# VectorE and ScalarE in the written order in two stages of a two-block transformer on one core

## The chip, the cores and the metric

The kernel runs on one core of a Trainium2 chip. The metric is the device time of one execution in microseconds (us): the median of repeated runs, lower is better.

## What is computed

A chain of eight sub-layers on 256 tokens of width 1024 in f32: sparse attention, an MLP, forgetting attention, an MLP, a short convolution, an expert layer, differential attention and a second expert layer (`peer`, called twice). The change lies in the two expert layers. Each has 16,384 experts, addressed by two halves of 128 keys; a token takes 16 experts for each of 8 heads:

```python
def chunk(xc):
    q = (xc @ w_q).reshape(PEER_CHUNK, PEER_HEADS, 2, PEER_HALF)
    s = jnp.einsum('thpd,pnd->thpn', q, sub_keys)
    sv, si = lax.top_k(s, PEER_TOPK)
    cand_s = (sv[:, :, 0, :, None] + sv[:, :, 1, None, :]).reshape(...)
    cand_i = (si[:, :, 0, :, None] * PEER_KEYS + si[:, :, 1, None, :]).reshape(...)
    top_s, pos = lax.top_k(cand_s, PEER_TOPK)
    idx = jnp.take_along_axis(cand_i, pos, axis=-1)
    g = jax.nn.softmax(top_s, axis=-1)
    act = jax.nn.gelu(jnp.einsum('td,thkd->thk', xc, u[idx]), approximate=False)
    return jnp.einsum('thk,thkd->td', g * act, v[idx])
```

## The kernel before, in words

**Weights.** The weights of all stages stream through one queue of chunks of 128x1024 f32 (512 KB). SP's queue loads each into a `raw` buffer (three, and a fourth where the stage has room). `Weights.prep` (L296-319) splits a chunk into two parts: ScalarE casts the high part `whi` (L316), VectorE subtracts it from `raw` for the low part `wlo` (L317). `next` prepares up to three chunks ahead of the one in use. TensorE's `prod` multiplies a chunk in 24 matmuls: eight k-blocks of `whi` with the high and the low part of the activations (L527, L528: 16), then eight of `wlo` with the high part (L530). So a chunk needs the ScalarE cast first, and the VectorE difference only after 16 matmuls.

**The expert layer.** `begin` normalizes the input and makes the first four products early, while the normalization's factors are still computed; their results are corrected by `right` (L1399, L1419, tile `bo`). `peer_route` then multiplies 16 query chunks (`raw<-w_pq`, 256 tokens wide), and behind each of them two chunks of the experts' first matrix (`raw<-u`, `u_chunk`, 224 tokens wide; the last 32 tokens go by gathers of rows). 128 such chunks are needed; `u_chunk` applies the GELU to the result on ScalarE (L1810; once gates are there also L1817 with a product on VectorE, L1818). The query result is copied (L1760), its scores follow on TensorE one product later (`score`, L1750), and for every second query, that is for a head, ScalarE copies the scores to `sc` (L1753). Behind the third query, ScalarE adds the residual (L1279).

**The selection** is a generator in the background: each `project` lets it go on by one step, behind its product. A head takes six steps: `best` (L1654 to L1658: maximum, index, replacement, maximum, index on VectorE) for each of two token halves and two key halves, and per token half a step that forms candidate sums (L1671, L1672) and picks the best of them. Behind the eight heads comes `choose` for each token half in 14 steps: the softmax (L1685 to L1709, Exp on ScalarE), and the picked indices by comparison, product and sum on tiles of 128x1024 (L1718, L1721, L1722), four times; then three transposes on TensorE (L1730) and copies. `u_chunk` is called until the generator is done.

**Behind it** come the gates (L1919 to L1953) for the first 224 tokens, beside the remaining first-matrix chunks, and a side generator `gathered` (L1864 to L1916) that gathers rows for the last 32 tokens on POOL's queue and sums them on VectorE (L1893, L1907; these keep their own order by `keep_in_program_order`).

**The value stage.** For each of 128 chunks of the second matrix (`raw<-v`, `SA<-v`), `split` casts the row of gated activations into a high part (ScalarE L1973) and a low part (VectorE L1974), one row ahead, and TensorE multiplies it with the chunk in 8 matmuls of 448 columns and 8 of 224 (L2017) into eight banks.

**What sets the order.** The kernel is written as one stream of instructions. A scheduler orders each engine's share of it by its own estimates of durations and dependencies; the stream's order binds it only through data and buffers, and where the kernel pins instructions. Each engine runs its queue in the order that results. `manual_schedule(engines=...)` is a region of that scheduler: within it, each engine of the set issues its instructions in the order written. Other engines (TensorE, POOL, SP), the order across engines, and the place of the region's instructions among those of the same engine from outside, stay the scheduler's.

Of the kernel before, what the change touches and what calls it, by code (L numbers as in the profile page):

```python
# [32 lines left out]
LAMBDA_INIT = 0.8 - 0.6 * math.exp(-0.3)  # L33
NEG = -1e30
PER_Q = 2

GATHER = (32, 32)

# [316 lines left out]
class Kernel:  # L355
# [1281 lines left out]
    def peer_route(self, l, x, n_in, it, jt, g1, g2, pool, u_chunk, picked):  # L1637
# [22 lines left out]
        def tops():  # L1660
            for h in range(8):
                sc = scs.pop(h)
                for t in range(NT):
                    for p in range(2):
                        best(sv[t][:, 2 * h + p], si[t][:, 2 * h + p], sc[:, t, p])
                        yield


                    v0, v1 = sv[t][:, 2 * h], sv[t][:, 2 * h + 1]
                    cand = pw.tile([128, 136], F32, name="cand", bufs=2)  # L1670
                    nc.vector.tensor_scalar(cand[:, 0:16], v1, v0[:, 0:1], None, op0=ALU.add)  # L1671
                    nc.vector.tensor_add(cand[:, 16:].rearrange("p (r c) -> p r c", c=8),  # L1672
                                         v0[:, 1:16, None].to_broadcast([128, 15, 8]),
                                         v1[:, None, 0:8].to_broadcast([128, 15, 8]))
                    best(tss[t][:, h], poss[t][:, h], cand)
                    yield
            for t in reversed(range(NT)):
                yield from choose(t)
# [76 lines left out]
        for hp in range(16):  # L1755
# [5 lines left out]
            self.at(1, score, hp, q)  # L1761
            for _ in range(PER_Q):
                u_chunk()
            if hp == 1:
                self.background(tops(), 6 / (2 + 2 * PER_Q))

    def peer(self, l, inp):
# [4 lines left out]
        x, n_in = inp  # L1772
# [3 lines left out]
        with ExitStack() as es:  # L1776
            self.phase(g=4, f=4)
            with ExitStack() as s1:
# [4 lines left out]
                it = p0.tile([128, ND, 2], F16, name="it")  # L1783
                jt = p0.tile([128, ND, 2], F16, name="jt")
                g1 = p0.tile([128, ND, 2], F16, name="g1")
                g2 = p0.tile([128, ND], F32, name="g2")
# [17 lines left out]
                def u_chunk():  # L1804
                    j = done[0]
                    z = self.project(x, 0, ND)
                    tg = gated[0]
                    s = SA[:, j] if j < J3 else SB[:, j - J3]
                    if tg < ND:
                        nc.scalar.activation(s[:, tg:], z[:, tg:ND], AF.Gelu)  # L1810
                    if tg:
                        if tg < ND:
                            y = pact.tile([128, ND], F32, name="act", bufs=2)
                        else:

                            y = (it, jt)[j % 2].rearrange("p t a -> p (t a)").bitcast(F32)
                        nc.scalar.activation(y[:, :tg], z[:, :tg], AF.Gelu)  # L1817
                        nc.vector.tensor_mul(s[:, :tg], y[:, :tg], s[:, :tg])  # L1818
                    done[0] += 1

                with ExitStack() as s2:
                    self.lnp = self.wk = self.pool("pel", 1, stack=s2)
                    self.begin(inp)
                    self.w.widen(s2, count=60)
                    pr = self.pool("per", 1, stack=s2)
                    self.iota = self.const(pr, "iota")
                    nc.vector.tensor_copy(iof, self.iota)
                    self.peer_route(l, x, n_in, it, jt, g1, g2, pr, u_chunk, picked)
                    while self.bg is not None:
                        u_chunk()  # L1830
                        if self.bg_done:
                            self.bg = None
                    self.flush_tails()
                    assert self.w.used >= self.w.limit
                p3 = self.pool("pe3", 1, stack=s1)
                SB = p3.tile([128, NJ - J3, ND], F32, name="SB")
# [132 lines left out]
                def split(j):  # L1969

                    s = SA[:, j] if j < J3 else SB[:, j - J3]
                    c = pw.tile([128, 2, ND], F32R, name="c", bufs=3)
                    nc.scalar.copy(c[:, 0], s)  # L1973
                    nc.vector.tensor_sub(c[:, 1], s, c[:, 0])  # L1974
                    return c.rearrange("p a t -> p (a t)")


                cs = [split(0)]
                while done[0] < NJ:
                    u_chunk()  # L1980
# [3 lines left out]
                def added(m):  # L1984
                    add(m, ((out[m][:, 0:ND], 0), (out[m][:, ND:2 * ND], 0), (out[m][:, 2 * ND:2 * ND + G], ND)))
# [10 lines left out]
                for j0 in range(NJ - last + 1):  # L1996
                    if j0 == NJ - 8:
                        self.side_end()

                        inp = (self.xtile("xa"), 2) if l == 0 else None  # L2000
                        add = self.norm_tiles(1 + 2 * l, inp)
                    else:
                        self.tick()
                    if j0 == 24:
                        self.w.lengthen(self.wk, 2, NJ - j0)
                    js = range(j0, j0 + 1 if j0 < NJ - last else NJ)
                    ws = []
                    for j in js:
                        if j < NJ - 1:
                            cs.append(split(j + 1))  # L2010
                        ws.append(self.w.next())

                    def piece(i, part, m, start, stop):
                        o = out[m]
                        wm = ws[i][part][:, m * 128:m * 128 + 128]
                        n = 2 * ND - part * ND
                        nc.tensor.matmul(o[:, :n], wm, cs[i][:, :n], start=start, stop=stop, skip_group_check=True)  # L2017

                    if len(js) == 1:
                        for part in range(2):  # L2020
                            for m in range(KT):
                                piece(0, part, m, j0 == 0 and part == 0, False)
                        cs.pop(0)
                    else:
                        for m in range(KT):
                            for i in range(last):
                                for part in range(2):
                                    piece(i, part, m, False, i == last - 1 and part == 1)
                            if m > 0:
                                self.step()  # L2030
                                added(m - 1)
# [8 lines left out]
    def build(self):  # L2040
        nc, a = self.nc, self.a

        def w(name):
            return [a[name][j] for j in range(a[name].shape[0])]
# [4 lines left out]
        def wu(l):  # L2049
            q, u = w(f"w_pq{l}"), w(f"u{l}")  # L2050
            return [c for i in range(16) for c in [q[i]] + u[i * PER_Q:(i + 1) * PER_Q]] + u[16 * PER_Q:]

# [59 lines left out]
```

## Time and profile before

| | us |
|---|---|
| median of 3 runs (lowest, highest) | 2671.16 (2669.37, 2672.81) |
| the profiled execution | 2667.2 |
| its span in the trace | 2665.4 |
| TensorE busy in the span | 2550.9 |
| VectorE busy | 2061.5 |
| ScalarE busy | 1491.8 |
| routing of the first expert layer (first products to the last step of the choice) | about 855 to 1082 |
| routing of the second | about 1845 to 2070 |
| value stages begin at | about 1318 and 2305 |

The span is the time from the first to the last instruction in the trace. A busy TensorE (PE) includes matmuls at the lower clock. In the rows below, PEld is TensorE's weight load, DVE is VectorE, ACT is ScalarE, POOL is GpSimd and SP is SyncE; `wlo<-raw,whi` reads "tile wlo computed from raw and whi", L317 is a line of the kernel, x4 is a count of instructions, and a bracket at the end of a row gives the idle time of the engine ahead of it and what ended that.

### The profile page before, as it was taken

Reading aid. Unit: us, or ns where it says so; the run is one execution under the profiler, and the core shown is the slowest. Engines: PE = TensorE matmul, PEld = TensorE weight load, DVE = VectorE, ACT = ScalarE, POOL = GpSimd, SP = SyncE. Lnnn points to the kernel's source line nnn. Section 1 sums busy time; section 2 is a strip of 40 time slices with the busy share of each in tenths; the row PEclk is TensorE's granted clock in tenths of the full one; section 3 lists DMA queues with packets and bytes.
Section 4 is the critical chain, followed back from the end, with each engine's and each line's share of the span. In section 5 each row is a group of like instructions: output and inputs, shape, how many; then the busy total and the mean of one; then the engine's idle time right before and its main releaser. Section 6 shows DMA issues by size and latency. Waiting matters only on the chain. (4 is left out here: it accounts for less than half of the span.)

```text
span 2665.4 us, 50896 instructions
## 1 busy us (share of the span) xinstructions
PE 2550.9 (96%) x19696; PEld 2413.5 (91%) x19696; DVE 2061.5 (77%) x4181; ACT 1491.8 (56%) x3008; POOL 220.1 (8%) x150
## 2 busy tenths in 40 slices
PE   8999999989999998999899999999988999999997
PEld 7689998889999898899899998888988999889997
DVE  7678776588778886699878876768886699777786
ACT  5556455455455444588545554666444688545554
POOL 0000000000000000000023330000000000122320
PEclk9999999999999998999999999999998999999999
DMA  5148775378874454566688885332544666688882
GB/s 174 48 137 272 271 252 182 97 238 286 283 264 142 150 183 136 181 201 197 198 299 302 305 291 166 126 105 96 174 151 144 205 200 195 217 294 307 295 292 91
DMA packets 151955, 542.82 MB, mean 204 GB/s; under 512 B 17360, under 2 KB 20368, under 8 KB 151712
## 3 DMA queue, kind: packets, MB, share of 16 engines
q1 hardware_dynamic: 132600, 472.04, 53.8%
q0 software_dynamic: 18816, 67.25, 7.2%
q8 instruction: 154, 2.52, 0.4%
q14 instruction: 89, 0.73, 0.1%
q10 hardware_dynamic: 296, 0.28, 0.0%
HBM read 538.39 MB, written 1.11 MB: 202 GB/s over the span
## 5 line engine op out<-in xcount | busy, mean ns | idle before, releaser
L316 ACT CAST whi<-raw 128x1024 fp32r<-128x1024 f32 x715 | 749.0, 1048 | 761.3 <-PE g L528 321.3
L317 DVE TENSOR_TENSOR wlo<-raw,whi 128x1024 fp32r<-128x1024 f32 x715 | 868.7, 1221 | 365.2 <-ACT whi L316 345.2
L527 PE MATMUL g<-xa_hi,whi 128*128 128x224 f32 (+2 forms) x3136 | 776.1, 287 | 9.8 <-ACT whi L316 6.4
L528 PE MATMUL g<-xa_lo,whi 128*128 128x224 f32 (+2 forms) x3136 | 760.2, 283 | 1.3 <-DVE xa_lo L1264 1.2
L527 PEld LDWEIGHTS g<-xa_hi,whi 128*128 128x128 f32 x3136 | 610.8, 195 | 16.0 <-ACT whi L316 7.5
L528 PEld LDWEIGHTS g<-xa_lo,whi 128*128 128x128 f32 x3136 | 611.4, 195 | 3.2 <-DVE xa_lo L1264 2.4
L2017 PE MATMUL g<-c,whi 128*128 128x448 f32 x2048 | 470.0, 369 | 21.3 <-DVE c L1974 8.7
L530 PE MATMUL g<-xa_hi,wlo 128*128 128x224 f32 (+2 forms) x3136 | 436.6, 282 | 40.0 <-DVE wlo L317 40.0
L530 PEld LDWEIGHTS g<-xa_hi,wlo 128*128 128x128 f32 x3136 | 400.0, 195 | 44.2 <-DVE wlo L317 44.0
L2017 PEld LDWEIGHTS g<-c,whi 128*128 128x128 f32 x2048 | 369.5, 190 | 47.2 <-DVE c L1974 11.1
L2017 PEld LDWEIGHTS g<-c,wlo 128*128 128x128 f32 x2048 | 272.5, 192 | 7.8
L2017 PE MATMUL g<-c,wlo 128*128 128x224 f32 x2048 | 276.4, 275 | 0.0
L1939 ACT ACTIVATE o<-oj,g 128x128 f16<-128x128 f16 x448 | 144.1, 408 | 2.6 <-DVE oj L1936 2.5
L1878 POOL DMA_INDIRECT row<-ur,ei x64 | 87.9, 1373 | 694.0 <-DVE dots L1893 485.9
L1878 POOL DMA_INDIRECT row<-v,ei x64 | 118.6, 1853 | 250.4 <-DVE xr L1907 216.9
L316 ACT CAST whi<-SA 128x1024 fp32r<-128x1024 f32 x79 | 83.0, 1051 | 93.9 <-PE g L2017 89.3
L317 DVE TENSOR_TENSOR wlo<-SA,whi 128x1024 fp32r<-128x1024 f32 x79 | 96.6, 1223 | 48.0 <-ACT whi L316 47.8
L527 PE MATMUL g<-g_hi,whi 128*128 128x272 f32 (+1 forms) x512 | 127.6, 285 | 0.0
L528 PE MATMUL g<-g_lo,whi 128*128 128x272 f32 (+1 forms) x512 | 127.6, 284 | 0.0
L1208 DVE CUSTOM_DVE_ANT_0 ada_raw<-ada_raw,silu 128x1024 f32<-128x1024 f32 x96 | 116.8, 1217 | 1.6 <-DMA ada_raw<-ada 1.5
L528 PEld LDWEIGHTS g<-g_lo,whi 128*128 128x128 f32 x512 | 96.4, 188 | 0.0
L527 PEld LDWEIGHTS g<-g_hi,whi 128*128 128x128 f32 x512 | 96.2, 188 | 0.0
(477 smaller groups left out, 3713.2 us busy)
## 6 DMA issues: line engine op xcount, KB each, us to landing
raw<-u SPq DMA_DIRECT2D x256, 512.0 KB, 4.0
raw<-v SPq DMA_DIRECT2D x177, 512.0 KB, 6.0
raw<-w SPq DMA_DIRECT2D x128, 512.0 KB, 4.5
ada_raw<-ada SPq DMA_DIRECT2D x96, 512.0 KB, 4.8
SA<-v SPq DMA_DIRECT2D x79, 512.0 KB, 6.1
raw<-w_pq SPq DMA_DIRECT2D x32, 512.0 KB, 3.5
raw<-w_fox SPq DMA_DIRECT2D x25, 512.0 KB, 4.4
raw<-w_conv SPq DMA_DIRECT2D x24, 512.0 KB, 4.3
```

The source lines that it names most:

```text
L316: nc.scalar.copy(hi, raw)
L317: nc.vector.tensor_sub(lo, raw, hi)
L527: nc.tensor.matmul(out, wk, x[0][:, k, n0:n0 + n], start=first and k == 0, stop=False)
L528: nc.tensor.matmul(out, wk, x[1][:, k, n0:n0 + n], start=False, stop=False)
L530: nc.tensor.matmul(out, w[1][:, k * 128:(k + 1) * 128], x[0][:, k, n0:n0 + n], start=False, stop=last and k == KT - 1)
L1208: nc.vector.tensor_tensor_reduce(raw, raw, silu, 1.0, 0.0, op0=ALU.mult, op1=ALU.add, accum_out=m[:, t:t + 1]))
L1878: nc.gpsimd.indirect_dma_start(out=t[:], out_offset=None, in_=rows[p][:, :], in_offset=bass.IndirectOffsetOnAxis(ap=ei[:, g, k:k + 1], axi ...
L1939: nc.scalar.activation(o2[:, t], oj[:, t], AF.Copy, scale=g2[:, t0 + t:t0 + t + 1])
L2017: nc.tensor.matmul(o[:, :n], wm, cs[i][:, :n], start=start, stop=stop, skip_group_check=True)
```

## The change

Two stretches of the two expert layers are put into a region in which VectorE and ScalarE keep the written order: the routing with the loop that finishes the choice, and the value stage from the first `split` (with the remaining first-matrix chunks) to its last eight chunks. The gates and the gathers' start lie between the two, outside. No instruction is added, taken away or changed.

```diff
+ORDERED = {mybir.EngineType.Activation, mybir.EngineType.DVE}
...
-                    self.peer_route(l, x, n_in, it, jt, g1, g2, pr, u_chunk, picked)
-                    while self.bg is not None:
-                        u_chunk()
-                        if self.bg_done:
-                            self.bg = None
-                    self.flush_tails()
+                    with self.tc.manual_schedule(engines=ORDERED):
+                        self.peer_route(l, x, n_in, it, jt, g1, g2, pr, u_chunk, picked)
+                        while self.bg is not None:
+                            u_chunk()
+                            if self.bg_done:
+                                self.bg = None
+                        self.flush_tails()
...
+                order = ExitStack()
+                order.enter_context(self.tc.manual_schedule(engines=ORDERED))
                 cs = [split(0)]
                 while done[0] < NJ:
                     u_chunk()
...
                 for j0 in range(NJ - last + 1):
                     if j0 == NJ - 8:
                         self.side_end()
+                        order.close()
```

## Rows read from the trace of the kernel before

**Rows 1.** The page: busy us, share of the span, instructions.

```profile
PE 2550.9 (96%) x19696; PEld 2413.5 (91%) x19696; DVE 2061.5 (77%) x4181; ACT 1491.8 (56%) x3008; POOL 220.1 (8%) x150
```

**Rows 2.** TensorE's waits, 855 to 1082, then 1845 to 2070: us, times, longest.

```profile
PE g L530 <- DVE wlo L317: 21.0, 11, 4.2
PE g L527 <- ACT whi L316: 2.2, 1, 2.2
...
PE g L530 <- DVE wlo L317: 19.0, 10, 4.2
PE g L527 <- ACT whi L316: 2.5, 1, 2.5
```

**Rows 3.** Windows: us; PE, PEld, DVE, ACT, POOL busy; PEclk, DMA share, GB/s.

```profile
1004.30:1011.10 6.80, 4.95 (x23) 4.96 (x24) 6.80 (x14) 3.29 (x6) 0.70 (x1) 0.50 0.26 83
1014.50:1028.20 13.70, 10.24 (x46) 9.98 (x47) 12.29 (x21) 3.34 (x6) 1.58 (x3) 0.50 0.38 116
1079.40:1082.80 3.40, 3.40 (x19) 3.40 (x18) 3.38 (x3) 0.74 (x2) 0.00 (x0) 0.50 0.47 157
...
1990.80:2004.40 13.60, 9.52 (x43) 9.25 (x44) 13.60 (x25) 7.46 (x11) 1.67 (x3) 0.50 0.29 81
2007.80:2014.70 6.90, 5.95 (x28) 5.95 (x29) 4.32 (x4) 1.85 (x3) 0.57 (x2) 0.51 0.71 222
2062.40:2069.30 6.90, 4.71 (x22) 4.71 (x23) 6.22 (x6) 1.41 (x2) 0.00 (x0) 0.51 0.34 98
```

**Rows 4.** Windows of one head, the choice and the stretch behind it.

```profile
893.80:912.20 18.40, 17.55 (x152) 17.37 (x152) 15.55 (x59) 8.43 (x13) 0.00 (x0) 1.00 0.52 173
...
1006.00:1030.00 24.00, 17.35 (x86) 16.90 (x87) 21.05 (x39) 9.66 (x14) 3.40 (x6) 0.61 0.37 118
1030.00:1070.00 40.00, 40.00 (x361) 40.00 (x361) 18.37 (x17) 18.83 (x31) 0.00 (x0) 1.00 0.52 170
```

**Rows 5.** VectorE's timeline in one head: start us, us, instruction.

```profile
902.56 0.28 DVE L1655 FIND_INDEX8 si<-sv,sc 128x8 uint32<-128x128 f32 x1
902.77 0.07 DVE L1655 MATCH_VALUE_LOAD si<-sv,sc 128x8 f32 x1
...
909.18 0.30 DVE L1654 MAX8 ts<-cand 128x8 f32<-128x136 f32 x1
909.52 0.09 DVE L1655 MATCH_VALUE_LOAD pos<-ts,cand 128x8 f32 x1
...
910.95 4.61 DVE L317 TENSOR_TENSOR wlo<-raw,whi 128x1024 fp32r<-128x1024 f32 x4
```

**Rows 6.** TensorE's timeline in the choice.

```profile
1006.15 2.05 PE L530 MATMUL g<-xa_hi,wlo 128*128 128x224 f32 x8 [3.93 <-DVE wlo L317]
...
1028.46 1.06 PE L530 MATMUL g<-xa_hi,wlo 128*128 128x224 f32 x8
```

**Rows 7.** VectorE's timeline in the choice.

```profile
1006.41 0.68 DVE L1721 TENSOR_TENSOR oh<-oh,sf 128x1024 f16<-128x1024 f16 x1
...
1007.12 1.22 DVE L1722 TENSOR_REDUCE pick<-oh 128x64 f32<-128x1024 f16 x1
...
1008.46 1.22 DVE L1718 TENSOR_TENSOR oh<-io,ra 128x1024 f16<-128x1024 f16 x1
```

**Rows 8.** ScalarE's timeline in one head.

```profile
902.76 1.05 ACT L316 CAST whi<-raw 128x1024 fp32r<-128x1024 f32 x1 [1.10 <-PE g L528]
903.71 0.35 ACT L1810 ACTIVATE SA<-g 128x224 f32<-128x224 f32 x1
```

**Rows 9.** Starts of the value stages: TensorE's and ScalarE's timelines.

```profile
1326.64 2.24 PE L2017 MATMUL g<-c,whi 128*128 128x448 f32 x5 [8.03 <-ACT jt L1817]
...
1322.65 1.99 ACT L316 CAST whi<-raw 128x1024 fp32r<-128x1024 f32 x2 [4.72 <-DMA raw<-v]
...
1326.25 0.34 ACT L1817 ACTIVATE jt<-g 128x224 f32<-128x224 f32 x1
...
2308.96 3.69 PE L2017 MATMUL g<-c,whi 128*128 128x448 f32 x8 [4.28 <-ACT whi L316]
```

## The prediction

> **What bounds the kernel now.** I read the busy shares first: TensorE is busy for 2550.9 of 2665.4 us and VectorE for 2061.5 [rows 1], so an edit that only reorders VectorE and ScalarE can give back at most what TensorE loses through them: idle time, and time at the lower of its two clock levels. The table of TensorE's waits comes second. In the two routing stretches its largest entry is the low part of a weight chunk (L317) that comes late for L530: 21.0 us in 11 waits in the first layer and 19.0 in 10 in the second, together 40.0, beside one wait for the high part (L316) of 2.2 and of 2.5 us, at the stages' starts [rows 2]. That is 44.7 us of idle TensorE. Third, the granted clock by stretch: six stretches behind the long waits of the choice stand at 0.50 to 0.51 of 2.4 GHz, that is at 1.2 GHz, with 18.6 us of TensorE work in the first layer's three and 20.2 in the second's [rows 3]. Eight L530 matmuls take 2.05 us there, behind a wait of 3.93 us, and 1.06 us at full clock [rows 6], so 0.48 of that work is lost time: 8.9 and 9.7 us. Idle and clock together are **63.3 us**.
>
> Fourth, why the low part is late. In the stretch of one head (six chunks) TensorE works 17.55 of 18.40 us and VectorE 15.55; in the expert choice VectorE works 21.05 of 24 us, and in the 40 us behind it 18.37, while TensorE is full [rows 4]. So VectorE has room on the whole, but not in the right places. Its timeline shows the scheduler's order: some 34 selection instructions of one head stand in one burst, up to 910.95, where four low parts follow in one go (4.61 us) [rows 5]: TensorE has then used up its lead of three chunks. In the choice both token halves' comparisons and sums stand in a row [rows 7].
>
> **The change, part by part.** No instruction is added or taken away, and no transfer: SP's and POOL's queues keep the scheduler's order. What moves is where VectorE and ScalarE place their work. A load on SP's queue goes out when a low part has freed its `raw` buffer, so spread low parts spread the loads as well; this is costed at nothing, and if loads came late in turn, the lead of three chunks would pay first.
>
> *Heads.* In the written order one step of the background generator follows each low part. Its price rises, because the bursts interleave two halves: an instruction that needs nothing from the one before follows 0.21 us later (902.56 to 902.77), a dependent one 0.34 us later (909.18 to 909.52) [rows 5]. A `best` alone runs from 909.18 to 910.95, 1.77 us. Six steps of a head are then 4 x 1.74 (a little less for the 128 columns of `sc`) + 2 x 2.2 (`cand` adds two short instructions) = 11.4 us, and six low parts at 1.15 (4.61 / 4) make 6.9: 18.3 us against TensorE's 17.55. VectorE falls behind by 0.75 us per head, 6.0 over eight heads. The cover is the lead: three chunks in preparation; a chunk is 24 matmuls at 0.111 us (361 in 40.00 us [rows 4]) = 2.7 us. About half of the 6.0 is covered if the stage is entered with a lead of one chunk; I take 3 us per layer, with 0 and 6 as ends.
>
> The rows above say that a dependent instruction comes 0.13 us later than an independent one. The Trainium skill (VectorE: DVE Perf Modes, "The DRAIN you can't avoid") says that the pipeline empties behind each operation in any case, and that eight copies took the same time with a semaphore behind each as with one behind the last; by that rule the written order would cost nothing more and the sum would be 6 us lower. The rows here differ, and the sum goes by them.
>
> *Choice.* A heavy pair of steps is a comparison (1.22 us), a low part, then a product (0.68; the sum starts 0.71 behind it), a sum (1.22) and a low part [rows 7]: at 1.15 for each of the long ones, as in the four low parts above, 2.3 + 3.0 = 5.3 us per two chunks, against 5.4 on TensorE. So it breaks even, and the light steps ahead of each half refill the lead. The waits of 3 to 4 us, the clock drop among them, should go.
>
> *Start of a stage.* The two waits for the high part are there, 4.7 us [rows 2]. The written order has its own late point: the high part of the second chunk falls behind the early products' copies on ScalarE. The trace of before doesn't show that; the bounds are 0 and twice the present 4.7 us; I take 2.5 us per layer, about what is there now.
>
> *ScalarE.* Today the high part starts when L528 has freed its buffer, ahead of the GELU of the same chunk (902.76 [rows 8]). Written, the GELU goes first: 8 matmuls (0.9) + 0.36 later. Behind the freeing come then 1.3 + 1.05 + one step of 1.74 + 1.22 = 5.3 us until the low part is there; TensorE asks for it 0.9 + 2.7 + 2.7 + 1.8 = 8.0 us behind. So 2.7 us of slack are left: nothing is charged.
>
> *Value stage.* The order is nearly the written one but for its start, where TensorE stands for 8.03 us (first layer) behind a GELU that ScalarE runs at 1326.25, behind two high parts, and for 4.28 us (second) for a high part [rows 9]. That high part waited for its transfer (4.72 <- DMA raw<-v), which the change does not move. Bounds: nothing, or a loss of a few us if the splits now wait in line, to 8.0 + 4.3 of gain. I take 3 us.
>
> **Sum.** 63.3 - 2 x 3 - 2 x 2.5 + 3 = 55 us. The profiled execution took 2667.2 us: 2612. The median of the runs shown is 4.0 above it: **2616 us**.
>
> **The rivals.**
> *VectorE becomes the bound* of heads and choice. For it: 18.3 against 17.55. Against it: the lead, and the same VectorE's 18.37 of 40 us right behind. Then the whole debt is paid, 6.0 in the heads and 8 x 0.3 for the steps with a product and a sum (3.0 against 2.7), 8.4 us a layer in place of 3: 11 us less gain, 2627.
>
> *A new wait on TensorE's side*: its order stays the scheduler's, and a transpose of the picks (L1730) or a score could stand ahead of products while VectorE now does that step later. Up to 4 us, four times: 2632. Against it: today's list has no such wait.
>
> *Slower: ScalarE's order couples the chunks.* Place: high part behind GELU, low part behind the step. It decides once 2.7 us of slack are used up, by later transfers, say; from there every chunk pays. A layer's routing has some 76 (48 with the queries, 28 for the steps of the choice); 55 us / 152 = 0.36 us each would cancel the gain, and 0.5 us each would give 2671 - 55 + 76 = 2692. Against it: the 2.7 us.
>
> *It does nothing*: the order isn't what holds the low parts, or the bursts only regroup and the same waits come up elsewhere. For it: transfers too come late in places (the 4.72 us above). Against it: the four low parts in one go. 2671, give or take 5.
>
> **How the numbers follow.** The forecast gets 0.60, VectorE's bound 0.21, the new wait 0.06, nothing 0.05, slower 0.08. A measurement of this kernel can tell about 0.2%, 5.3 us, from no change. Faster: 0.60 + 0.21 + 0.06 = 0.87; same 0.05; slower 0.08. The range: the forecast's upper gain is no debt, no wait at the starts and the whole value stage, 63.3 + 12.3 = 76, 2595, taken at 2594 for rounding; the other end takes in the two faster rivals (2627, 2632) and 12 us more where both come or the value stage loses, 2644. What is left out is the last two cases.
>
> **What would show it.** Right: the 40.0 us of L530 behind L317 fall under 15; the half-clock stretches of the choice are gone; the VectorE timeline of a head shows one low part, one `best`, one low part, with VectorE above 17 of 18 us; a head's period is near 17.6 to 18.3. VectorE's bound: waits of some tenths behind L317, many of them. Wrong: L527 waiting for the high part in every chunk, a period above 18.4, or the waits of 3 to 4 us still there. In the value stage the 8.03 us shrink or stay with the transfer.

## The result and the profile after

The change made the kernel faster: 2598.76 us (median of 4 runs, 2595.51 to 2599.11) against 2671.98 us for the kernel before on the same chip (4 runs), a ratio of 0.9723 with a 95% interval of 0.9706 to 0.974. That is 73 us where 55 were forecast; 2598.8 lies in the range of 2594 to 2644, near its lower end. The profiled execution has a span of 2593.7 us, 71.7 under that of before.

The first line of the page answers to [rows 1], the waits of the two routing stretches (851 to 1083 and 1802 to 2034) to [rows 2]:

```profile
PE 2528.2 (97%) x19696; PEld 2392.0 (92%) x19696; DVE 2090.1 (81%) x4181; ACT 1487.9 (57%) x3008; POOL 215.9 (8%) x150
```

```profile
PE g L532 <- DVE wlo L319: 1.2, 3, 0.4
PE g L529 <- ACT whi L318: 0.5, 2, 0.3
...
PE g L532 <- DVE wlo L319: 1.2, 3, 0.4
PE g L529 <- ACT whi L318: 0.3, 1, 0.3
```

(Two lines of code stand ahead of everything in the changed kernel: L317 is now L319, L530 is L532.) The 40.0 us behind the low part have become 2.4, the 4.7 us behind the high part 0.8. TensorE's busy time fell by 22.7 us with the same instructions, for the most part because the choice's matmuls no longer run at the lower clock (8.9 and 9.7 us by the prediction's count); VectorE's rose by 28.6 with the same instructions. The windows below show both stages: the first two are heads, the other two the choice; they answer to [rows 3, 4]:

```profile
890.00:907.60 17.60, 17.60 (x157) 17.60 (x156) 16.71 (x59) 8.62 (x15) 0.00 (x0) 1.00 0.51 172
...
942.80:960.40 17.60, 17.60 (x150) 17.25 (x149) 16.74 (x58) 8.32 (x13) 0.00 (x0) 1.00 0.52 177
...
1000.00:1020.00 20.00, 19.20 (x165) 18.56 (x165) 17.50 (x52) 11.64 (x17) 0.00 (x0) 1.00 0.56 186
1020.00:1040.00 20.00, 20.00 (x181) 20.00 (x181) 19.58 (x26) 9.01 (x15) 1.87 (x3) 1.00 0.57 182
```

The clock is 1.00 through the choice, where it had been 0.61 over 24 us. VectorE's timeline in a head has one low part, one `best`, one low part, and no idle time; the next `cand` step follows in the same way:

```profile
898.08 1.21 DVE L319 TENSOR_TENSOR wlo<-raw,whi 128x1024 fp32r<-128x1024 f32 x1
899.20 0.29 DVE L1656 MAX8 sv<-sc 128x8 f32<-128x128 f32 x1
899.52 0.09 DVE L1657 MATCH_VALUE_LOAD si<-sv,sc 128x8 f32 x1
...
900.92 1.21 DVE L319 TENSOR_TENSOR wlo<-raw,whi 128x1024 fp32r<-128x1024 f32 x1
902.04 0.23 DVE L1673 TENSOR_SCALAR cand<-sv 128x16 f32<-128x16 f32 x1
```

A table of the stretches (us), cut at the last early product, the last transpose of the choice and the first and last matmul of the value stage. The routings of the kernel before end at 1111.0 and 2097.5 by this cut, 29 and 27 us behind the windows of [rows 2]; TensorE has no wait in between:

| stretch | before | after | difference |
|---|---|---|---|
| routing, first layer | 260.9 | 231.5 | -29.4 |
| gates, first layer | 206.8 | 207.3 | +0.5 |
| value stage, first layer | 349.9 | 343.0 | -6.9 |
| routing, second layer | 262.5 | 231.4 | -31.1 |
| gates, second layer (the wait of 4.28 us ends it) | 211.5 | 207.2 | -4.3 |
| value stage, second layer | 341.7 | 338.1 | -3.5 |
| all else | 1032.3 | 1035.2 | +3.0 |

And inside the routing, from the use of one low part to another, counted from the end (74 uses): the first five intervals, 36 chunks of six heads, the rest with the choice. First layer 16.8, 109.9, 110.5 us before and 14.2, 106.9, 89.3 after; second layer 18.7, 109.5, 111.2 and 14.2, 106.6, 89.3. The choice gives over 21 us a layer, the heads 3, the start 2.6 to 4.5; another 2.6 and 1.8 us lie ahead of the first of these uses. Part of the start's gain is clock: between the last early product and the fifth interval TensorE did 6.2 and 9.6 us of work at 1.2 GHz before, 3.3 and 6.3 with the change.

**What the page doesn't show.** TensorE seems to be full in both head windows above, 17.60 of 17.60 us. But the first holds 157 matmuls and the second 150; that is no gap in the records, since the chunks themselves follow each other more slowly, as shown below. The distance from the end of each low part to its first use, worked out from the trace for the first 54 chunks of the first layer (us), tells why:

```
3.6 2.1 2.0 1.9 1.6 1.6 1.5 1.3 1.2 1.1 0.9 0.8 0.7 0.5 0.4 0.3 0.1 0.1 0.1 0.1 0.1 0.1 0.1 0.1 0.1 0.1 0.1
0.1 0.1 0.1 0.1 0.1 0.1 0.1 0.1 0.1 0.1 0.1 0.1 0.1 0.1 0.1 0.1 0.1 0.1 0.1 0.1 0.1 0.1 0.1 1.3 0.9 2.2 2.8
```

The lead is used up over 16 chunks; from then to the end of the heads every low part is used 0.1 us after it is made. VectorE sets the pace there. Three chunks (one query, two others) take 3.13 + 2.79 + 2.72 = 8.64 us on TensorE while there is a lead and 3.34 + 2.89 + 2.79 = 9.02 us afterwards: 17.28 and 18.04 us per head. VectorE's head measured here is 18.05 us (from the `cand` step at 893.01 to that at 911.06). The single waits are too short for the list of waits, which shows 1.2 us. Two of the L532 matmuls of one chunk start 0.23 and 0.21 us behind the one before (at 941.61 and 941.81), where 0.11 is usual, but the one before is shown as 0.28 and 0.37 us long, so no gap appears. The weight loads (PEld, the second column) show part of it: 17.60 us in the first window, 17.25 in the second.

The lead at the entry differs from run to run. In the five runs with the selections as here in an ordered routing (the change, and below the routing alone, VectorE alone, the gates and the region closed early) the six heads take 104.4 to 106.9 us; the 104.4 is the first layer with the routing alone in order, where the second distance is 4.5 us (2.1 in the list above) and the lead lasts for some 35 chunks. The choice takes 89.3 to 89.6 us in all of them.

### The profile page after: what moved, and what is told of

Read it like the earlier page. It is cut to its first block, busy times and chain, and to the rows that moved or that the text cites. A ratio compares the mean times of both kernels' runs of the same rounds, so it can differ in the third digit from the quotient of the medians.

```text
span 2593.7 us, 50917 instructions
## 1 busy us (share of the span) xinstructions
PE 2528.2 (97%) x19696; PEld 2392.0 (92%) x19696; DVE 2090.1 (81%) x4181; ACT 1487.9 (57%) x3008; POOL 215.9 (8%) x150
## 4 chain that ended last, share of the span: by engine, by line
PE 75%; DVE 16%; DMA 4%; ACT 4%; issue 1%; ACTq 0%; SPq 0%; DVEq 0%
PE g L2023 20%; PE g L529 12%; PE g L532 12%; PE g L530 12%; DVE wlo L319 7%; DMA raw<-v 3%; ACT whi L318 2%; PE g L609 1%; PE g L610 1%; PE g L1390 1%; PE g L611 1%; PE g L1392 1%; PE g L1391 1%; PE o L1146 1%; DVE si L1657 1%
## 5 line engine op out<-in xcount | busy, mean ns | idle before, releaser
L319 DVE TENSOR_TENSOR wlo<-raw,whi 128x1024 fp32r<-128x1024 f32 x715 | 871.5, 1220 | 245.3 <-ACT whi L318 237.3
L529 PE MATMUL g<-xa_hi,whi 128*128 128x224 f32 (+2 forms) x3136 | 762.7, 284 | 7.9 <-ACT whi L318 4.8
L530 PE MATMUL g<-xa_lo,whi 128*128 128x224 f32 (+2 forms) x3136 | 746.8, 279 | 0.5 <-DVE xa_lo L1266 0.4
L529 PEld LDWEIGHTS g<-xa_hi,whi 128*128 128x128 f32 x3136 | 600.9, 192 | 14.2 <-ACT whi L318 6.1
L530 PEld LDWEIGHTS g<-xa_lo,whi 128*128 128x128 f32 x3136 | 601.4, 192 | 2.0 <-DVE xa_lo L1266 1.3
L532 PE MATMUL g<-xa_hi,wlo 128*128 128x224 f32 (+2 forms) x3136 | 431.9, 280 | 2.4 <-DVE wlo L319 2.4
L532 PEld LDWEIGHTS g<-xa_hi,wlo 128*128 128x128 f32 x3136 | 391.9, 191 | 7.3 <-DVE wlo L319 3.5
L1942 ACT ACTIVATE o<-oj,g 128x128 f16<-128x128 f16 x448 | 144.1, 409 | 0.0
L1812 ACT ACTIVATE SA<-g 128x224 f32<-128x224 f32 (+19 forms) x188 | 65.1, 346 | 129.7 <-PE g L532 129.6
L319 DVE TENSOR_TENSOR wlo<-SA,whi 128x1024 fp32r<-128x1024 f32 x79 | 96.7, 1223 | 46.7 <-ACT whi L318 46.7
L530 PE MATMUL g<-g_lo,whi 128*128 128x272 f32 (+1 forms) x512 | 127.6, 284 | 0.0
L530 PEld LDWEIGHTS g<-g_lo,whi 128*128 128x128 f32 x512 | 96.4, 188 | 0.0
```

Of the source, the lines that this page charges most:

```text
L319: nc.vector.tensor_sub(lo, raw, hi)
L529: nc.tensor.matmul(out, wk, x[0][:, k, n0:n0 + n], start=first and k == 0, stop=False)
L530: nc.tensor.matmul(out, wk, x[1][:, k, n0:n0 + n], start=False, stop=False)
L532: nc.tensor.matmul(out, w[1][:, k * 128:(k + 1) * 128], x[0][:, k, n0:n0 + n], start=False, stop=last and k == KT - 1)
L1942: nc.scalar.activation(o2[:, t], oj[:, t], AF.Copy, scale=g2[:, t0 + t:t0 + t + 1])
```

## The experiments

Profiled spans are compared with 2665.4 (before) and 2593.7 us (the change); medians with their intervals stand beside them. Line numbers in the rows are those of each kernel.

**1. The routing alone, the value stage alone.** Either region was left out:

```diff
-                order.enter_context(self.tc.manual_schedule(engines=ORDERED))
+                pass
```

```diff
-                    with self.tc.manual_schedule(engines=ORDERED):
+                    with ExitStack():
```

> The region around the routing alone; the value stage in the scheduler's order. If the two stretches are independent and the routing carries the gain, the two routings lose 60 us together (29.4 + 31.1 in the trace of the changed kernel) and the start of the value stages keeps its waits of 8.0 and 4.3 us: a profiled span near 2606 us. Rival: part of what the value stage gained (about 14 us with the end of the gates) comes from an earlier end of the routing; then the value stages get shorter here too and the span is near 2594.

> The region around the value stage alone. If the parts are independent: about 10 to 14 us less than before (span near 2652), the 8.0 us wait behind the GELU gone, all routing waits of before (40 us behind L317) still there. Rival: the value stage's gain needs the ordered routing; then the span stays within 3 us of before.

Routing alone: 2607.36 us, ratio 0.978 (0.9747 to 0.9812), span 2602.4; the routings are 30.9 and 31.7 us shorter. Its value stages begin as before, with a wait of 7.32 us behind the GELU and one of 3.87 for the high part. Value stage alone: 2664.99 us, ratio 0.9978 (0.9962 to 0.9994), span 2659.5, with 44.7 us behind the low part. So the two are nearly independent: by medians 64.6 us and 7.0 us, 71.6 together, against 73. The value stage expected at 10 to 14 us was too high; the table above credits it with some 14, but with the routing alone the second value stage was already 3.0 us shorter, without a region there. That much is scatter between kernels, and 7 to 9 us (2607.36 - 2598.76 = 8.6) is what the region is worth. All profiles of this document together say where: with ScalarE in order the first value stage takes 343.0 to 347.1 us and the second gates 207.2 to 207.3, otherwise 348.0 to 350.8 and 210.4 to 211.5 (kernels with the gates in order aside); the second value stages overlap.

**2. One engine at a time**, in both stretches:

```diff
-ORDERED = {mybir.EngineType.Activation, mybir.EngineType.DVE}
+ORDERED = {mybir.EngineType.DVE}
```

and the same with `Activation` alone.

> Both stretches, but VectorE alone keeps the written order; ScalarE stays the scheduler's. Theory: the routing's gain is the low parts spread between the selection steps, on VectorE alone: at least 45 of the 60 us stay, the waits behind L317 fall under 10 us, and the 8.0 us wait of the first value stage, which is ScalarE's order, may stay. Rival: ScalarE's order decides as well (high parts early, late low parts in front of a full VectorE); then under 30 us of gain.

> Both stretches, but ScalarE alone keeps the written order. Theory: the bursts on VectorE stay, so the waits of the choice (seven to eight of 3 to 4 us) and the lower clock behind them stay; the gain is the value stage's alone and the starts' waits for the high part, 5 to 20 us, or a loss where high parts now come behind the GELU and the low parts behind a burst. Rival: ScalarE carries the gain: over 40 us.

VectorE alone: 2608.47 us, ratio 0.9775 (0.9746 to 0.9805). The routings are 30.7 and 30.3 us shorter: all of their gain is VectorE's order. ScalarE alone: 2669.86 us, ratio 1.0001 (0.9987 to 1.0015). TensorE's waits there:

```profile
PE g L532 <- DVE wlo L319: 55.0, 22, 5.9
```

They are 15 us longer than [rows 2]: in each head the wait grew to 1.48 us (heads before: 0.6 to 1.0). The high part now stands behind the GELU while the low parts still stand behind bursts; that this is the reason was not tried by itself. The routings are only 3.2 and 2.8 us longer, and about as much is gained elsewhere: what ScalarE's order does give is the start of the value stage. Its first 18 us in the first layer, before, with the full change, with VectorE alone and with ScalarE alone:

```profile
1317.00:1335.00 18.00, 9.97 (x48) 9.05 (x48) 9.22 (x14) 6.22 (x11) 1.87 (x2) 0.72 0.59 199
```

```profile
1289.00:1307.00 18.00, 16.39 (x106) 15.30 (x106) 14.05 (x21) 8.35 (x15) 4.07 (x3) 1.00 0.83 273
```

```profile
1289.00:1307.00 18.00, 12.05 (x71) 11.17 (x70) 10.17 (x17) 7.41 (x13) 2.92 (x2) 0.81 0.57 193
```

```profile
1319.00:1337.00 18.00, 16.28 (x104) 14.84 (x102) 14.33 (x22) 8.56 (x16) 4.00 (x3) 1.00 0.77 270
```

48 matmuls before, 106 and 104 with ScalarE in order, 71 with VectorE alone. The granted clock comes back as well, from 0.72 to 1.00 here and from 0.77 (2303 to 2318) to 1.00 (2240 to 2255) in the second layer: before, TensorE did 5.4 and 6.1 us of work at 1.2 GHz at the two starts, with the change none. ScalarE's timeline of the changed kernel answers to [rows 9]: the GELU (L1819) goes ahead of the split and of the high parts that wait for transfers:

```profile
1290.37 0.36 ACT L1819 ACTIVATE jt<-g 128x224 f32<-128x224 f32 x1 [1.39 <-PE g L532]
1290.62 0.37 ACT L1976 CAST c<-SA 128x224 fp32r<-128x224 f32 x1
1291.05 1.05 ACT L318 CAST whi<-raw 128x1024 fp32r<-128x1024 f32 x1
...
1293.79 1.05 ACT L318 CAST whi<-raw 128x1024 fp32r<-128x1024 f32 x1 [0.44 <-DMA raw<-v]
```

The transfers are still late in places: the next wait for one, at 1307.25, is 3.50 us long. ScalarE's waits for them in the whole first value stage, 22.0 us in 8 before, are these with the change:

```profile
ACT whi L318 <- DMA raw<-v: 19.2, 12, 3.5
```

But no GELU stands behind such a wait now, and TensorE's list of the stage names neither the GELU nor a high part. With VectorE alone in order ScalarE keeps the scheduler's order, the GELU comes behind two high parts and a wait of 5.08 us for a transfer, and TensorE waits 5.95 us for it.

**3. Heads alone, choice alone.** The region covers either the call of `peer_route` or the loop behind it; in both kernels the value stage has no region, so they compare with the routing alone (2607.36 us). The first edit, cut short:

```diff
                     with self.tc.manual_schedule(engines=ORDERED):
                         self.peer_route(l, x, n_in, it, jt, g1, g2, pr, u_chunk, picked)
-                        while self.bg is not None:
-                            u_chunk()
...
+                    while self.bg is not None:
+                        u_chunk()
...
-                order.enter_context(self.tc.manual_schedule(engines=ORDERED))
```

> The region around the routing up to the last query, so that starts and most of the heads are in the written order; the end of the choice and the value stage are the scheduler's. If the gain is made where the waits were: starts and heads give what they gave in the full change, 5.6 us in the first layer and 7.4 in the second, span near 2652; the choice keeps its waits of 3 to 4 us. Rival: the choice's waits come from what the heads leave behind; then they shrink too and the span is under 2640.

> The region only around the loop that finishes the last head and makes the choice. Expected: the choice gives its 21.2 and 21.9 us, span near 2622; the heads keep their period of 18.1 to 18.6 us. Rival as for the heads alone, from the other side: under 30 us of gain.

The first did not come out as expected (span 2662.4 against 2652), the second nearly (2625.5 against 2622). Heads alone: 2665.8 us, ratio 0.9975 (0.9961 to 0.9988). Start and heads are as short as in the full change or nearly so (14.2 and 107.3 us; 14.2 and 108.8), but the choice has grown from 110.5 to 116.1 and from 111.2 to 115.1 us. Its waits:

```profile
PE g L532 <- DVE wlo L319: 38.7, 10, 5.4
```

The rival had a dependence in it, with the sign turned: ordered heads leave no lead, so the burst of the choice costs more (5.4 us at the longest, 4.2 in [rows 2]). Choice alone: 2624.47 us, ratio 0.9805 (0.9778 to 0.9831); its choice takes 86.6 us, 2.7 less than in the full change, again because it begins with the lead that the scheduler's heads leave. So of the routing's gain the choice alone brings four fifths (23.8 and 25.0 us shorter routings, of 29.4 and 31.1), and ordered heads cost nearly as much in the choice (2.7 us a layer) as they give in the changed kernel (3.0); what is left is the start's.

**4. Is VectorE the bound in the heads?** Load was added, and then the price taken away. In the first kernel each `best` on the scores is followed by two copies that nothing reads:

```diff
+        spare = pw.tile([128, 128], F32, name="spare", bufs=1)
...
                         best(sv[t][:, 2 * h + p], si[t][:, 2 * h + p], sc[:, t, p])
+                        for _ in range(2):
+                            nc.vector.tensor_copy(spare, sc[:, t, p])
                         yield
```

In the second the selections are written in pairs, two independent ones alternating, half of both in one step and half in the next; each has `max`, `max_index`, `match_replace`, `max`, `max_index` as before:

```diff
+        def first(jobs):
+            for vals, idx, src in jobs:
+                nc.vector.max(vals[:, 0:8], src)
+            for vals, idx, src in jobs:
+                nc.vector.max_index(idx[:, 0:8], vals[:, 0:8], src)
...
                 for t in range(NT):
-                    for p in range(2):
-                        best(sv[t][:, 2 * h + p], si[t][:, 2 * h + p], sc[:, t, p])
-                        yield
+                    jobs = [(sv[t][:, 2 * h + p], si[t][:, 2 * h + p], sc[:, t, p]) for p in range(2)]
+                    first(jobs)
+                    yield
+                    second(jobs)
+                    yield
...
```

(the two `cand` selections of a head are paired in the same way).

> The changed kernel with two more copies of 128x128 on VectorE in each selection step of the heads (128 per layer; nothing reads them). In the changed kernel VectorE's head takes 18.05 us against 17.28 on TensorE, and the low parts are ready only 0.1 us ahead of their use from the 18th chunk on. If VectorE is the bound there, the copies go into the time nearly whole: at 0.15 to 0.2 us each 19 to 26 us per layer, 38 to 52 in all, less what is left of the lead (under 2 us), so 32 to 50 us more than the changed kernel. Rival: TensorE, which the page shows as fully busy there, is the bound; then under 15 us.

> The changed kernel with the selection steps written so that two independent selections alternate instruction by instruction, half of both in one step and half in the next; same instructions, same number of steps. VectorE's head should fall from 18.05 towards 15.6 us (the time the scheduler's interleaved bursts take), under TensorE's 17.28; the heads' period then falls from 18.04 to 17.28 where VectorE was the bound, 4.2 us per layer, 8 us in all: span near 2585. Rival: VectorE is not the bound, or the alternating steps pay the same price: no change within 3 us.

With load: 2627.92 us, ratio 0.9832 (0.9807 to 0.9857), 29.2 us more than the change by the medians and 30.7 by the spans. The routings are 11.3 and 11.9 us longer than in the changed kernel, 23.2 together; nearly all of the rest is in the value stages, which have no load and scatter by as much from kernel to kernel. The expectation had miscounted: four steps of a head with two copies are 8 per head and 64 per layer, not 128. At its 0.15 to 0.2 us that is 10 to 13 us a layer, and the measured 11 to 12 lie in it: VectorE's added work goes into the time nearly whole, and the rival (under 15 us in all) falls. A head window holds 138 matmuls:

```profile
940.00:957.60 17.60, 16.74 (x138) 15.89 (x138) 16.64 (x62) 7.01 (x11) 0.00 (x0) 1.00 0.47 151
```

In pairs: **2589.91 us**, ratio 0.9691 (0.9671 to 0.9711), span 2586.1 where 2585 was expected. That is 8.9 us under the change by the medians, though the intervals of the two ratios touch; the routings tell them apart. They take 226.3 and 225.4 us here and 225.4 to 226.4 in the two other kernels with pairs (experiment 6), against 230.0 to 232.2 in the five ordered kernels with chains: some 5 us a layer. VectorE works 15.34 us in a head window that now holds 157 matmuls, with idle time ahead of its low parts, and a `match_replace` pair stands 0.27 us apart (941.71, 941.98):

```profile
940.00:957.60 17.60, 17.60 (x157) 17.60 (x156) 15.34 (x61) 8.61 (x14) 0.00 (x0) 1.00 0.57 180
```

```profile
940.57 1.23 DVE L319 TENSOR_TENSOR wlo<-raw,whi 128x1024 fp32r<-128x1024 f32 x1 [0.29 <-ACT whi L318]
941.71 0.09 DVE L1670 MATCH_VALUE_LOAD sc<-sv,sc 128x8 f32 x1
941.78 0.28 DVE L1670 MATCH_REPLACE8 sc<-sv,sc 128x128 f32<-128x128 f32 x1
941.98 0.08 DVE L1670 MATCH_VALUE_LOAD sc<-sv,sc 128x8 f32 x1
```

The heads take 103.5 us in both layers (3.4 and 3.1 less than with the change) and the choice 86.6 (2.7 less): 6.1 and 5.8 us were the price of VectorE's longer chain in the two layers of the changed kernel. Where the routing alone is ordered and the lead at the entry is larger, it is 3.6 and 5.5 us.

**5. Where the written order loses: the gates.** The second region begins ahead of the gates:

```diff
+                order = ExitStack()
+                order.enter_context(self.tc.manual_schedule(engines=ORDERED))
                 p3 = self.pool("pe3", 1, stack=s1)
...
-                order = ExitStack()
-                order.enter_context(self.tc.manual_schedule(engines=ORDERED))
                 cs = [split(0)]
```

> The changed kernel with the second region begun ahead of the gates, so that routing, gates and value stage are all in the written order. TensorE waits only 3.0 + 1.3 us in the gates' 207 us of the first layer, so little is to be gained: 0 to 4 us per layer if the scheduler's order was no better than the written one there. Rival: VectorE (191 of 207 us busy) and ScalarE (166) are so full there that an order bound to the text makes them wait for each other: 10 us or more lost.

2912.04 us, ratio 1.0902 (1.0879 to 1.0926): 313 us more than the change. The two gates' stretches grew from 207 to 363 and 364 us. TensorE's waits:

```profile
PE f L1947 <- DVE o L1942: 164.2, 103, 3.2
```

Only half of the loss is such idle time: TensorE idles 84 and 85 us in the two stretches, 80 each more than with the change. The granted clock falls too. A window over the first gates, with the change and then here:

```profile
1083.00:1290.00 207.00, 202.72 (x1977) 198.08 (x1976) 191.01 (x404) 166.03 (x498) 18.91 (x17) 0.99 0.65 201
```

```profile
1083.00:1466.00 383.00, 296.91 (x2086) 266.01 (x2086) 218.24 (x427) 180.99 (x515) 21.12 (x20) 0.86 0.37 122
```

In each of the two stretches TensorE did 104 to 105 us of work at 1.2 GHz, 3.4 and none with the change; with the 0.48 that [rows 6] give, that is an estimate of 50 us a layer. The last 26 or so are not settled. One group of tokens:

```profile
1156.43 1.23 DVE L319 TENSOR_TENSOR wlo<-raw,whi 128x1024 fp32r<-128x1024 f32 x1 [0.73 <-ACT whi L318]
1157.58 0.42 DVE L1940 TENSOR_TENSOR oi<-iof,it 128x512 f16<-128x512 f16 x1
1157.91 0.42 DVE L1941 TENSOR_TENSOR oj<-iof,jt 128x512 f16<-128x512 f16 x1
...
1158.42 1.28 ACT L1944 ACTIVATE o<-oj,g 128x128 f16<-128x128 f16 x4 [2.02 <-DVE oj L1941]
1158.84 0.23 PE L1947 MATMUL f<-o,oi 128*128 128x128 f16 x1 [1.92 <-DVE o L1942]
...
1160.01 0.48 DVE L1954 SCALAR_TENSOR_TENSOR SA<-f,SA 128x312 f32<-128x312 f32 x1 [1.22 <-PE f L1948]
```

Here a step of the text is a chain over three engines: VectorE's comparisons and a first product (L1942), ScalarE's four scalings, TensorE's eight matmuls, VectorE's last product. In the written order each engine waits for the link before its own, TensorE 1.92 us for the product of L1942 here, and the next low part is behind VectorE's wait for TensorE. In the scheduler's order a comparison of the next group is made ahead (L1939 at 1201.53 in the changed kernel, behind the product of the group before at 1200.99), and TensorE has this wait only twice in the first gates (3.0 us).

**6. Two variants.** The paired selections with the side generator's GELU and product written in jobs 1 and 3 of the next group of sums (before: in job 15 of its own and in job 1 of the next):

```diff
-                            if k == 15:
-                                nc.scalar.activation(dots[:, g], dots[:, g], AF.Gelu)
-                            if k == 1 and g > 0:
+                            if k == 1 and g > 0:
+                                nc.scalar.activation(dots[:, g - 1], dots[:, g - 1], AF.Gelu)
+                            if k == 3 and g > 0:
...
```

and the same with the gates in the written order.

> The alternating selections, and in the side generator of the value stage the GELU of a group of sums and its product with the weights are written one and three jobs later. In the changed kernel ScalarE stands 3.68 and 2.44 us at that GELU for VectorE's sum, with the next row's split behind it; TensorE then waits 1.61 us for the split once. Expected: those two ScalarE waits gone, 1 to 4 us less than the alternating selections alone (span near 2584). Rival: the split's waits come from VectorE's own row sums in front of it (1.2 us each); then no change within 2 us.

> The same with the gates in the written order too. The sum of what the two others show if the parts are independent: the span of the former plus the difference that the gates' region makes to the changed kernel.

2588.59 us, ratio 0.9688 (0.967 to 0.9706), not to be told from 2589.91 (the profiled execution, the longest of its five, has a span of 2593.0 where 2584 was expected): ScalarE's two waits at that GELU are gone in the first layer's value stage, TensorE's waits for the split are 14.9 us where they were 12.5. That is the rival's side: the waits for the split come from elsewhere; from where was not tried. The last kernel took 2899.39 us, 1.0853 (1.0833 to 1.0874): the gates' loss is the same 311 us.

**7. The value stage's region closed after six chunks.**

```diff
+                    if j0 == 6:
+                        order.close()
                     if j0 == NJ - 8:
                         self.side_end()
-                        order.close()
```

> The changed kernel with the value stage's region closed after six chunks; the other 122 are the scheduler's. If the value stage's gain is made where TensorE stood before, at its start, the span stays within 4 us of the changed kernel's 2593.7 and the first 18 us of the value stage hold about 105 matmuls as there (48 before). Rival: the written order of the later chunks carries a part; then the stage is 5 us or more longer than in the changed kernel (343.0 and 338.1 us).

2598.93 us, ratio 0.9721 (0.9704 to 0.9739), the same as the change's 2598.76. The profile is less clear: its span of 2598.4 is 4.7 us above the change's, just past the 4 expected, and the start held 92 matmuls in 18 us, fewer than 105. The value stages were 4.1 and 1.6 us longer, while the routings were shorter by 1.4 each. By the medians the order of the later chunks brings nothing that can be told, so the region's gain is most likely made at the start.

## Why the prediction was right, and where it was off

**The mechanism held.** The low parts stood behind VectorE's bursts; spread between the steps they are in time. VectorE's order alone gives the routing's gain (30.7 and 30.3 us), ScalarE's alone none of it. The clock came back with the waits, as the 1.00 windows of the choice show.

**The sum was too small by 18 us**, in these terms:

- *Idle and clock, 63.3.* It was read from the list of waits and is an undercount. With the paired selections the routings are 34.6 and 37.1 us shorter than before, 71.7 together, so at least that was lost. A part is what the busy time hides: a head takes 103.5 / 6 = 17.25 us on TensorE without any wait, not the 17.55 of [rows 4], so 0.3 us per head lay in "busy" (some 5 us in the 16 heads). Another part is the clock at the starts of the routings, which [rows 3] don't cover: 6.2 and 9.6 us of TensorE's work ran at 1.2 GHz there, 3.3 and 6.3 with the change, 1.4 and 1.6 us by the same 0.48. With their shorter waits that makes 5.0 us a layer of the 5.2 and 6.3 that the starts give with the change; what is left is not settled.
- *Heads, 3 us a layer, ends 0 and 6.* The debt of 0.75 us per head was right (18.04 - 17.28 = 0.76), and so was the 18.3 us of VectorE's head nearly (18.05). The step that failed is "about half of the 6.0 is covered": the lead pays for the first 16 chunks, but is then missing at the choice. What it saved in the heads is lost there, and the debt is paid in full, about 6 us in the changed kernel's profile. It is 3.6 us in the layer whose lead lasts longest (the first with the routing alone), so a larger lead covers up to 2.5 of the 6 us.
- *Starts, 2.5 us a layer.* No new wait appeared: the first five intervals fell to 14.2 us in both layers. The high part behind the early products' copies was not late, and the eight residual instructions (L1281) now stand one by one between the high parts.
- *Choice.* Break-even was right: low parts stay ahead, 0.7 to 4.0 us before their use. The stretch gave 21.2 and 21.9 us, and 23.9 and 24.6 where it begins with a lead, against 14.6 + 8.9 and 14.6 + 9.7 us of waits and clock counted.
- *ScalarE, nothing charged.* The four terms 0.9 + 2.7 + 2.7 + 1.8 make 8.1 us and not 8.0, so the slack is 2.8; nothing hangs on it, and the waits for a high part in the routings stay at 0.3 us or less.
- *Value stage, 3 us.* It gave 7 to 9. The step that failed is to let the gain hang on the transfer ("That high part waited for its transfer, which the change does not move"). The transfers still come late, but the GELU for which TensorE stood no longer comes behind the high parts that wait for them: with ScalarE alone in order TensorE does 104 matmuls in place of 48, with VectorE alone 71. The clock at the two starts, 5.4 and 6.1 us of work at 1.2 GHz, was not in the sum either.

**The rivals.** VectorE's bound came true in the heads, half hidden: the forecast had set "VectorE above 17 of 18 us" as right and "waits of some tenths, many of them" as the rival's sign, and neither the list of waits nor the busy share showed it; the count of matmuls per window and the distance of each low part from its use did. The rule of the Trainium skill (VectorE: DVE Perf Modes, "The DRAIN you can't avoid"), by which a chain costs no more than the same operations without waits, would have made the debt zero, and so the time 6 us shorter; the paired selections, the same operations, are some 5 us a layer faster, so the rule does not hold for them. The same section of the Trainium skill also says "A next op that is not held starts earlier", for instructions with no wait between them, which the forecast left out. The rows fit that: 0.21 us between independent instructions, 0.34 between dependent ones [rows 5]. No new wait on TensorE's transposes appeared in the list. The slower rival did not come at the place it named: ScalarE's order alone lengthened the head's wait to 1.48 us, but beside VectorE's order nothing is left of it. Where the written order does couple the engines is the gates, which the change leaves out.

## What to carry to other kernels

As far as this kernel shows, take the order from the text only where the text puts small, independent steps between the urgent instructions; where one step is a chain over several engines, leave it to a scheduler that works ahead, or write the work ahead by hand. In an ordered stretch the text also decides whether dependent short instructions stand back to back: alternate two independent chains. When an engine looks full, count its instructions per window and look at how long before its use each input is ready.

## What the runs showed of the hardware that was not expected

A TensorE that the page shows as busy for 17.60 of 17.60 us did 150 matmuls in one window and 157 in another at the same granted clock of 1.00: the chunks follow each other 0.07 to 0.21 us later, and a matmul that is shown as 0.28 us long while the next usually starts 0.11 us behind it leaves no gap for that. On VectorE the same 34 selection instructions of a head (as the kernel writes them; the trace shows 52 rows) take 18.05 - 6 x 1.12 = 11.3 us as dependent chains and some 8.8 us as the scheduler's interleaved burst, all without a wait for another engine.
